# A decoder block with two token mixers: convolution taps summed in PSUM, one bank per chunk for the recurrence, and one merge for all chunks

## The chip, the cores and the metric

The kernel runs on one core of a Trainium2 chip. A core has a matrix engine (PE, with weight loads shown apart as PEld), a vector engine (DVE), an activation engine (ACT), a general engine (POOL) and an engine that here only issues DMAs (SP). SBUF is the working memory; PSUM is the small memory in eight banks that PE writes its products to. Each engine runs its own instructions in the order in which they were written for it.

The metric is the device time of one execution in microseconds (us), as the median of several runs. A lower time is better.

## The reference

One residual block on x (2048 tokens of 1024 channels), in float32. All widths are 1024, the recurrence has 16 heads of 64.

```python
h = _rmsnorm(x, norm_g) * (1 + scale) + shift           # scale, shift, gate from c
p = h @ w_in                                            # 1024 -> 9344
c_val, c_gate, c_og, ts, r_og, g_conv, g_rwkv = split(p)

# branch A: gated causal depthwise convolution of width 31
u = c_val * sigmoid(c_gate)
u = causal_depthwise_conv(u, conv_k) + conv_b
y_conv = (silu(layernorm(u)) * silu(c_og)) @ w_conv_out

# branch B: RWKV-7, per head a 64 x 64 state
r, k, v, w_low, a_low = split(token_shift(ts))
state = state * w_t - (state @ kk_t) b_t^T + v_t k_t^T  # for each token t
o_t = state @ r_t
y_rwkv = ((groupnorm(o) + (r * k * r_k).sum() * v) * silu(r_og)) @ w_rwkv_out

m = sigmoid(g_conv) * y_conv + sigmoid(g_rwkv) * y_rwkv
out = _rmsnorm(x + gate * (m @ w_out), final_g)
```

## The kernel before

**Tiling.** The 2048 tokens are worked in 4 blocks of 512 (b). In a block, the normalised input lies as 8 tiles of 128 channels by 512 tokens, each split into a high and a low part, so that a product of float32 is three fast matmuls (mm3k, L173). Within a block, the 16 heads are worked in 4 groups (g) of 4 heads, two pairs of heads each; so there are 16 groups in all.

**A group** (function group) does the following in turn.
1. pair (L420), once for each of the two pairs, makes the decayed keys and queries of the 8 chunks of 64 tokens (KR, BK, tk) and the matrices between tokens of a chunk (As). uv holds the values, and later the solution beside them.
2. The inverse. Each chunk needs the inverse of a unit triangular 64 x 64 matrix. Its two 32 x 32 diagonal blocks are sent through DRAM (dA, then La) so that 128 of them lie one to a partition, two for each block. POOL runs 31 steps of elimination, each a product (L568) and a sum (L570) on 1 to 16 rows. The results go back through DRAM (dT, L574) into As by 16 DMAs on SP's queue (L581).
3. The merge (L583 to L610) makes the off-diagonal block. For e = 0 and 1 (even and odd chunks lie in different partitions): 16 transposes of 32 x 32 on DVE (T11, L591), 16 small matmuls into the bank late (L597), a copy to SBUF (Qs, L600), 16 more matmuls into late (L606), and two copies into As (L610). The pool pl has one bank under the tag late, which xnorm's transposes and the group's own output transposes (L683) use as well.
4. The chain over the chunks (L615 to L656). In chunk c: Se is the decayed state (ACT, L621); xo = KR x state (L624) plus the values' part (L629); X is its copy to SBUF by DVE (L632); the solution gd = inverse x X (L637); uv = gd x rn by DVE (L639); the state's update from tk x uv (L643) and four DVE instructions (L648); last the output o, added by matmuls to the other half of xo (L654), and copied by ACT into O (L656). xo has two buffers (pool px), gd has one bank of its own (pool pg). The next chunk needs the new state.
5. Group normalisation and the transposes of the output (L669 to L686).

**The convolution** (function conv) is run 8 times a block. Two projections give gate and value, u is their gated product with 30 tokens of history in front (L711). DVE sums the 31 taps: the first writes the tile yj in SBUF (L714), and 30 instructions each add one tap in place (L717). yj has one buffer and goes to DRAM by a DMA of SP (L719).

**Order.** The code is written group by group, with the convolutions and gate projections (fill) behind or between the parts of a group. A planner then orders the instructions of each engine once and for all, by priority, by when it reckons their inputs to be ready, and by free buffers. So the projections (L173) are laid between the steps of the chain, and the next group's pairs, inverse and transposes between the chunks of the one before. Where an input comes later than planned, the engine stands, and everything behind it on that engine with it. After the blocks a second phase (L850 on) makes the output projections.

The banks of PSUM during the blocks: pm 2 (main products), pa 2 (aux), px 2 (xo), pl 1 (late), pg 1 (gd).

Of the kernel before, what the change touches and what calls it, by code (L numbers as in the profile page):

```python
# [9 lines left out]
F32 = mybir.dt.float32  # L10
# [8 lines left out]
P = 128  # L19
# [63 lines left out]
def hybrid_block(ctx: ExitStack, tc: tile.TileContext, x, vecs, convk, w2a2, final_g, ada, w_in, w_co, w_ro, w_o, crow, out,  # L83
# [137 lines left out]
    pg = late.enter_context(tc.tile_pool(name="pg", bufs=1, space=PSUM))  # L221
# [120 lines left out]
    def hprep0(xs, ada_steps):  # L342
# [17 lines left out]
        for k in range(KT):  # L360
            next(ada_steps)
            pt = (pl, pg)[k % 2].tile([P, NTT, P], F32, name="ps_x", tag=("late", "gd")[k % 2])
# [52 lines left out]
    def vrow(e):  # L415
        return slice(0, 64) if e == 0 else slice(64, 128)
# [118 lines left out]
    def group(b, g, h, lora, fill):  # L535
# [48 lines left out]
        Qs = lt.tile([P, 2, 2, NCH // 2, 32], F32, name="Qs", tag="i2")  # L584
        for e in range(2):
            p0 = 64 - 64 * e
            lo_, hi_ = slice(p0, p0 + 32), slice(p0 + 32, p0 + 64)
            for q in range(2):
                for hh in range(2):
                    for c in range(NCH // 2):  # L590
                        nc.vector.transpose(T11[lo_, q, hh, c, :], As[q][lo_, hh, 2 * c + e, lo_])  # L591
            pq = pl.tile([P, 2, 2, NCH // 2, 32], F32, name="late", tag="late")
            n = 0
            for q in range(2):
                for hh in range(2):
                    for c in range(NCH // 2):
                        nc.tensor.matmul(pq[hi_, q, hh, c, :], As[q][lo_, hh, 2 * c + e, hi_], T11[lo_, q, hh, c, :],  # L597
                                         start=(n == 0), stop=(n == 15), skip_group_check=True)
                        n += 1
            nc.vector.tensor_copy(Qs[hi_], pq[hi_])  # L600
            pf = pl.tile([P, 2, 2, NCH // 2, 32], F32, name="late", tag="late")
            n = 0
            for q in range(2):
                for hh in range(2):
                    for c in range(NCH // 2):
                        nc.tensor.matmul(pf[lo_, q, hh, c, :], Qs[hi_, q, hh, c, :], As[q][hi_, hh, 2 * c + e, hi_],  # L606
                                         start=(n == 0), stop=(n == 15), skip_group_check=True)
                        n += 1
            for q in range(2):
                nc.vector.tensor_copy(As[q][lo_, :, e::2, hi_], pf[lo_, q])  # L610
# [3 lines left out]
        Sg = S[g]  # L614
        for c in range(NCH):  # L615
# [474 lines left out]
```

## Time and profile before

| | |
|---|---|
| median of 3 runs | 3379.35 us (3379.3 to 3392.31) |
| the profiled execution, its own time | 3373.04 us |
| its span, first to last instruction | 3371.3 us |
| mean granted clock of PE | 0.959 |
| instructions | 65315 |
| moved by DMA | 606.98 MB, mean 180 GB/s |

The span is the stretch from the first to the last instruction; the time of the execution has 1.7 us around it. In the profile a row of a group reads: line, engine, operation, tile written, arrow, tiles read, shape, count, then busy us and the mean ns of one, then the idle time of the engine just before such instructions and what ended it. An arrow with a name behind an idle time says whom the engine waited for. In the rows of stretches a number in brackets is a count of instructions. In the order of time, a row has its start, its length, and in square brackets the idle time before it. The four instruction names that matter most below are T (the tile T11), late (the merge's bank), yj (the taps) and gd, X, xo, uv, S (the chain). The tile's name there lacks its number, so T11 is T.

### The profile page before, as it was taken

The numbers are of one execution on the slowest core, as the hardware profiler recorded it, in microseconds if no ns is written. First come the engines' busy times: TensorE is split into PE (matmuls) and PEld (weight loads), VectorE is DVE, ScalarE is ACT, GpSimd is POOL, SyncE is SP. The second block draws the span as 40 slices with busy tenths as digits, with TensorE's granted clock in tenths as the row PEclk, the third lists the DMA queues.
The fourth block names the chain that finished last, engine by engine and source line by source line (L and its number), as shares of the span: only waits on it lengthen the run. The fifth ranks groups of instructions, "written<-read, shape, count | busy, mean of one in ns | idle before, by whom it ended". The sixth has DMA issues, their size and how long they took to land.

```text
span 3371.3 us, 65315 instructions
## 1 busy us (share of the span) xinstructions
PE 3110.2 (92%) x25664; PEld 2874.4 (85%) x25664; DVE 2378.0 (71%) x4712; ACT 1063.8 (32%) x1900; POOL 1587.6 (47%) x2158
## 2 busy tenths in 40 slices
PE   6889898999999989999999899999989898878998
PEld 5789898888899988898989898989989877667887
DVE  7786777776677665767666567757688656889755
ACT  4432433332223131323232314132322223344422
POOL 3375454534544535253636355727576413746201
PEclk9999999999999999899999999999999999898999
DMA  7765656663546465445554556646446655655543
GB/s 295 243 210 181 230 174 222 222 197 119 177 142 190 140 184 166 148 132 174 159 155 150 182 165 215 211 124 186 158 127 200 217 181 188 216 184 177 179 158 124
DMA packets 328468, 606.98 MB, mean 180 GB/s; under 512 B 130848, under 2 KB 147552, under 8 KB 328160
## 3 DMA queue, kind: packets, MB, share of 16 engines
q1 hardware_dynamic: 265088, 373.14, 33.7%
q0 software_dynamic: 63072, 229.67, 22.0%
q8 instruction: 202, 3.31, 0.4%
q14 instruction: 106, 0.87, 0.1%
HBM read 439.03 MB, written 162.53 MB: 178 GB/s over the span
## 4 chain that ended last, share of the span: by engine, by line
PE 46%; DVE 18%; POOL 15%; DMA 11%; issue 6%; SPq 2%; ACT 2%; POOLq 0%; DVEq 0%; ACTq 0%
PE ps_main L173 30%; POOL TT L570 5%; POOL itmp L568 5%; DVE yj L717 5%; PE aux L504 3%; DMA As<-dT 2%; DMA dT<-TT 2%; DMA La<-dA 1%; PE gd L637 1%; PE xo L654 1%; PE xo L629 1%; DMA dA<-As 1%; POOL w_lo L158 1%; PE gd L643 1%; PE pout L1007 1%
## 5 line engine op out<-in xcount | busy, mean ns | idle before, releaser
L173 PE MATMUL ps_main<-h_hi,w_hi 128*128 128x256 f32 x4608 | 981.0, 290 | 39.8 <-DVE th L700 18.0
L173 PE MATMUL ps_main<-h_hi,w_lo 128*128 128x256 f32 x4608 | 973.5, 289 | 26.4 <-POOL w_lo L158 24.4
L173 PE MATMUL ps_main<-h_lo,w_hi 128*128 128x256 f32 x4608 | 964.9, 288 | 0.2 <-DVE h_lo L328 0.2
L717 DVE SCALAR_TENSOR_TENSOR yj<-u,ck,yj 128x512 f32<-128x512 f32 x960 | 802.3, 836 | 21.8
L173 PEld LDWEIGHTS ps_main<-h_hi,w_hi 128*128 128x128 f32 x4608 | 732.0, 193 | 60.4 <-issue 21.5
L173 PEld LDWEIGHTS ps_main<-h_hi,w_lo 128*128 128x128 f32 x4608 | 730.7, 193 | 40.5 <-POOL w_lo L158 27.0
L173 PEld LDWEIGHTS ps_main<-h_lo,w_hi 128*128 128x128 f32 x4608 | 730.1, 193 | 8.2 <-issue 1.2
L568 POOL TENSOR_TENSOR itmp<-La,TT 128x126 f32<-128x126 f32 (+22 forms) x496 | 274.2, 553 | 105.1 <-DMA La<-dA 73.5
L156 ACT CAST w_hi<-w_st 128x1024 fp32r<-128x1024 f32 x167 | 175.5, 1051 | 446.5 <-DMA w_st<-w_in_t 114.7
L570 POOL TENSOR_TENSOR TT<-TT,itmp 128x126 f32<-128x126 f32 (+22 forms) x496 | 279.5, 564 | 32.7
L149 POOL DMA_DIRECT2D w_hi<-kh_in x219 | 126.8, 579 | 348.5 <-PE ps_main L173 323.9
L158 DVE TENSOR_TENSOR w_lo<-w_st,w_hi 128x1024 fp32r<-128x1024 f32 x120 | 162.9, 1357 | 132.8 <-PE ps_main L173 50.3
L648 DVE SCALAR_TENSOR_TENSOR S<-gd,pe,Se 64x64 f32<-64x64 f32 x512 | 144.7, 283 | 91.6 <-PE gd L643 82.6
L158 POOL TENSOR_TENSOR w_lo<-w_st,w_hi 128x1024 fp32r<-128x1024 f32 x47 | 117.8, 2506 | 94.8 <-ACT w_hi L156 91.2
L656 ACT COPY uv<-xo 64x256 f32<-64x256 f32 x128 | 47.1, 368 | 342.6 <-PE xo L654 270.4
L506 DVE TENSOR_TENSOR As<-aux,maskA 128x512 f32<-128x512 f32 x128 | 88.3, 691 | 86.1 <-PE aux L504 85.8
L1018 POOL TENSOR_TENSOR xt<-xt,tg 128x256 f32<-128x256 f32 x60 | 52.8, 901 | 199.2 <-DVE tg L1014 192.0
L522 POOL TENSOR_TENSOR vv<-rk,vv 128x512 f32<-128x512 f32 x32 | 45.2, 1412 | 210.6 <-PE aux L519 152.5
L504 PE MATMUL aux<-KR,BKz 128*128 128x128 f32 x1024 | 138.2, 279 | 3.1 <-ACT rk L492 2.3
L504 PEld LDWEIGHTS aux<-KR,BKz 128*128 128x128 f32 x1024 | 125.2, 191 | 7.3 <-ACT rk L492 2.8
L591 DVE STREAM_TRANSPOSE T<-As 32x32 f32<-32x32 f32 x512 | 58.0, 166 | 102.7 <-DMA As<-dT 101.5
L632 DVE COPY X<-xo 64x256 f32<-64x256 f32 x128 | 53.7, 420 | 102.8 <-PE xo L629 101.5
(293 smaller groups left out, 5867.1 us busy)
## 6 DMA issues: line engine op xcount, KB each, us to landing
w_hi<-kh_in POOLq DMA_DIRECT2D x219, 512.0 KB, 4.0
w_lo<-kl_in POOLq DMA_DIRECT2D x219, 512.0 KB, 5.1
w_st<-w_in_t SPq DMA_DIRECT2D x73, 512.0 KB, 4.6
kh_in<-w_hi SPq DMA_DIRECT2D x71, 512.0 KB, 3.1
kl_in<-w_lo SPq DMA_DIRECT2D x71, 512.0 KB, 3.9
w_st<-w_ro_t SPq DMA_DIRECT2D x32, 512.0 KB, 4.0
w_st<-w_co_t SPq DMA_DIRECT2D x32, 512.0 KB, 3.8
w_st<-w_o_t SPq DMA_DIRECT2D x32, 512.0 KB, 3.6
```

Of the source, the lines that this page charges most:

```text
L149: nc.gpsimd.dma_start(hi, back[0])
L156: nc.scalar.copy(hi, st)
L158: lo_eng.tensor_tensor(out=lo, in0=st, in1=hi.bitcast(F32), op=ALU.subtract)
L173: nc.tensor.matmul(ps[:, qs], ww[:, k, :], aa[k][:, qs], start=(k == 0 and t == 0 and q == 0), stop=(k == KT - 1 and t == 2 and q == ms - ...
L504: nc.tensor.matmul(pA[:, c // 2, es], BKz[:, hh, cc, es], KR[:, cc, es], start=(c == 0), stop=(c == 3), skip_group_check=True)
L506: nc.vector.tensor_tensor(out=Asb[:, hh, c4 * 4:c4 * 4 + 4, :].rearrange("p (a e) n -> p a (e n)", e=2), in0=pA, in1=flat(maskA).unsqueeze ...
L568: nc.gpsimd.tensor_tensor(out=tmp[:, :ni, :nt], in0=La[:, j:j + 1, j + 1:].broadcast_to([P, ni, nt]), in1=TT[:, :ni, j:j + 1].broadcast_to ...
L570: nc.gpsimd.tensor_tensor(out=TT[:, :ni, j + 1:], in0=TT[:, :ni, j + 1:], in1=tmp[:, :ni, :nt], op=ALU.add)
L591: nc.vector.transpose(T11[lo_, q, hh, c, :], As[q][lo_, hh, 2 * c + e, lo_])
L632: nc.vector.tensor_copy(X[pr_], xo[pr_])
L648: nc.vector.scalar_tensor_tensor(out=Sg[hs, q, hs], in0=gd[hs, 2 + q, hs], scalar=R[q]["pe"][hs, c:c + 1], in1=Se[hs, q, hs], op0=ALU.mult ...
L717: nc.vector.scalar_tensor_tensor(out=yj, in0=u[:, i:i + TB], scalar=ck[:, j, i:i + 1], in1=yj, op0=ALU.mult, op1=ALU.add)
```

## The change

Four edits in the same diff.

- **Taps.** A pool pc of one PSUM bank takes the place of pg. The first tap writes its tile acc, the next 29 add in place in acc, and the last reads acc and writes yj in SBUF. The transposes of the first block (hprep0), which borrowed pg's bank, borrow acc's.
- **One bank per chunk.** xo grows from two to four columns blocks of 128, which is a whole bank. The solution and the state's update, which were in gd, now go into xo: the solution over the part that X was copied from, the update into the two new blocks.
- **Output.** The matmuls and the copy of o are put into a function olast, which is called for chunk c in chunk c + 1, between the copy to X and the solution, and after the loop for the last chunk.
- **Merge.** The loop over e that held everything is split into stages, each for both e: first all transposes, now one for four chunks at a time (32 x 128 instead of four of 32 x 32); then 32 matmuls; two copies to Qs; 32 matmuls; four copies into As. All of it uses one tile in late.

```diff
-    pg = late.enter_context(tc.tile_pool(name="pg", bufs=1, space=PSUM))
+    pc = late.enter_context(tc.tile_pool(name="pc", bufs=1, space=PSUM))
...
-            pt = (pl, pg)[k % 2].tile([P, NTT, P], F32, name="ps_x", tag=("late", "gd")[k % 2])
+            pt = (pl, pc)[k % 2].tile([P, NTT, P], F32, name="ps_x", tag=("late", "acc")[k % 2])
...
+        def quarters(e):
+            p0 = 64 - 64 * e
+            return slice(p0, p0 + 32), slice(p0 + 32, p0 + 64)
+        every = [(q, hh, c) for q in range(2) for hh in range(2) for c in range(NCH // 2)]
+        pq = pl.tile([P, 2, 2, NCH // 2, 32], F32, name="late", tag="late")
         for e in range(2):
-            p0 = 64 - 64 * e
-            lo_, hi_ = slice(p0, p0 + 32), slice(p0 + 32, p0 + 64)
+            lo_, hi_ = quarters(e)
             for q in range(2):
                 for hh in range(2):
-                    for c in range(NCH // 2):
-                        nc.vector.transpose(T11[lo_, q, hh, c, :], As[q][lo_, hh, 2 * c + e, lo_])
-            pq = pl.tile([P, 2, 2, NCH // 2, 32], F32, name="late", tag="late")
...
+                    nc.vector.transpose(T11[lo_, q, hh], As[q][lo_, hh, e::2, lo_])
+        for e in range(2):
+            lo_, hi_ = quarters(e)
+            for n, (q, hh, c) in enumerate(every):
+                nc.tensor.matmul(pq[hi_, q, hh, c, :], As[q][lo_, hh, 2 * c + e, hi_], T11[lo_, q, hh, c, :],
+                                 start=(n == 0), stop=(n == 15), skip_group_check=True)
+        for e in range(2):
+            lo_, hi_ = quarters(e)
+            nc.vector.tensor_copy(Qs[hi_], pq[hi_])
+        for e in range(2):
+            lo_, hi_ = quarters(e)
+            for n, (q, hh, c) in enumerate(every):
+                nc.tensor.matmul(pq[lo_, q, hh, c, :], Qs[hi_, q, hh, c, :], As[q][hi_, hh, 2 * c + e, hi_],
+                                 start=(n == 0), stop=(n == 15), skip_group_check=True)
+        for e in range(2):
+            lo_, hi_ = quarters(e)
+            for q in range(2):
+                nc.vector.tensor_copy(As[q][lo_, :, e::2, hi_], pq[lo_, q])
...
+        def olast(c, xo):
+            vr, rc = vrow(c % 2), rcol(c % 2)
             for q in range(2):
                 for hh in range(2):
+                    hs = slice(64 * hh, 64 * hh + 64)
+                    nc.tensor.matmul(xo[vr, q, hs], As[q][:, hh, c, rc], uv[:, c, q, hs],
+                                     start=False, stop=(q == 1 and hh == 1), skip_group_check=True)
+            nc.scalar.copy(O[vr, c // 2], xo[vr, 0:2])
...
-            xo = px.tile([P, 2, P], F32, name="xo", tag="xo")
+            xo = px.tile([P, 4, P], F32, name="xo", tag="xo")
...
-            nc.vector.tensor_copy(X[pr_], xo[pr_])
-            gd = pg.tile([P, 4, P], F32, name="gd", tag="gd")
+            nc.vector.tensor_copy(X[pr_], xo[pr_, 0:2])
+            if prev:
+                olast(*prev)
...
-                    nc.tensor.matmul(gd[pr_, q, hs], As[q][pr_, hh, c, kcol(e)], X[pr_, q, hs],
+                    nc.tensor.matmul(xo[pr_, q, hs], As[q][pr_, hh, c, kcol(e)], X[pr_, q, hs],
...
-                nc.tensor.matmul(gd[:, 2 + q, :], R[q]["tk"][:, c, :], uv[:, c, q, :], start=(q == 0), stop=(q == 1),
+                nc.tensor.matmul(xo[:, 2 + q, :], R[q]["tk"][:, c, :], uv[:, c, q, :], start=False, stop=(q == 1),
...
-            for q in range(2):
-                for hh in range(2):
-                    hs = slice(64 * hh, 64 * hh + 64)
-                    nc.tensor.matmul(xo[vr, q, hs], As[q][:, hh, c, rcol(e)], uv[:, c, q, hs],
-                                     start=False, stop=(q == 1 and hh == 1), skip_group_check=True)
-            nc.scalar.copy(O[vr, cc], xo[vr])
+            prev = (c, xo)
+        olast(*prev)
...
-        nc.vector.tensor_scalar(out=yj, in0=u[:, HALO:], scalar1=ck[:, j, HALO:HALO + 1], scalar2=vc("conv_b", j),
+        acc = pc.tile([P, TB], F32, name="acc", tag="acc")
+        nc.vector.tensor_scalar(out=acc, in0=u[:, HALO:], scalar1=ck[:, j, HALO:HALO + 1], scalar2=vc("conv_b", j),
                                 op0=ALU.mult, op1=ALU.add)
         for i in range(HALO):
-            nc.vector.scalar_tensor_tensor(out=yj, in0=u[:, i:i + TB], scalar=ck[:, j, i:i + 1], in1=yj,
-                                           op0=ALU.mult, op1=ALU.add)
+            nc.vector.scalar_tensor_tensor(out=acc if i + 1 < HALO else yj, in0=u[:, i:i + TB],
+                                           scalar=ck[:, j, i:i + 1], in1=acc, op0=ALU.mult, op1=ALU.add)
```

More of the change, by code (lines that the diff above doesn't have):

```diff
@@ L594, in group @@
+        O = uv[:, 0::2]
+        Sg = S[g]
+        prev = None
+        def olast(c, xo):
+            vr, rc = vrow(c % 2), rcol(c % 2)
             for q in range(2):
                 for hh in range(2):
[L596 to L599, printed above, removed]
@@ L600, in group @@
-            nc.vector.tensor_copy(Qs[hi_], pq[hi_])
-            pf = pl.tile([P, 2, 2, NCH // 2, 32], F32, name="late", tag="late")
-            n = 0
-            for q in range(2):
-                for hh in range(2):
[L605 to L608, printed above, removed]
```

11 lines of the change are left out of this document (2 added, 9 removed).

## The prediction

> **What bounds the kernel now.** I read the page first: the share of each engine, then PE over the span, then the chain that ended last.
>
> ```profile
> span 3371.3 us, 65315 instructions
> ...
> PE 3110.2 (92%) x25664; PEld 2874.4 (85%) x25664; DVE 2378.0 (71%) x4712; ACT 1063.8 (32%) x1900; POOL 1587.6 (47%) x2158
> ...
> PE   6889898999999989999999899999989898878998
> ...
> PE 46%; DVE 18%; POOL 15%; DMA 11%; issue 6%; SPq 2%; ACT 2%; POOLq 0%; DVEq 0%; ACTq 0%
> ```
>
> PE is busy 3110 of 3371 us, and no matmul is added or dropped by the change. So whatever the other engines win, the time can fall only by idle time of PE, 261 us in all. The second view is the busy time by stretch, to see where that idle time lies. The columns are PE, PEld, DVE, ACT and POOL busy, the clock, and DMA.
>
> ```profile
> 0.00:152.00 152.00, 111.35 (x848) 102.46 (x848) 105.52 (x232) 68.74 (x116) 42.04 (x46) 0.98 0.75 272
> 152.00:2700.00 2548.00, 2400.41 (x21473) 2257.91 (x21473) 1802.40 (x3755) 752.95 (x1369) 1310.30 (x1936) 0.96 0.56 175
> 2700.00:3371.00 671.00, 598.43 (x3345) 514.06 (x3344) 470.11 (x727) 242.08 (x416) 235.24 (x176) 0.94 0.53 177
> ```
>
> Taps, inverse, merge and the chunk chain run between 152 and 2700 us (the last chain ends a little later). There PE idles 2548 - 2400 = 148 us. The 41 us at the start and the 73 us at the end are of code that the change hardly touches. So about 148 us is at stake, 4.4% of the span. The third view is the waits of PE:
>
> ```profile
> PE gd L643 <- DVE uv L639: 24.9, 7, 9.2
> PE ps_main L173 <- POOL w_lo L158: 24.4, 13, 4.6
> ...
> PE ps_main L173 <- DVE th L700: 18.0, 5, 10.4
> PE late L597 <- DVE T L591: 15.9, 9, 3.3
> PE aux L249 <- ACT rh L490: 12.4, 6, 6.6
> ...
> PE ps_main L173 <- DVE carry L401: 9.1, 8, 1.9
> ...
> PE gd L637 <- DVE X L632: 6.7, 6, 2.9
> PE xo L624 <- DVE S L648: 6.4, 5, 3.8
> ```
>
> Columns: total us, times, longest. The largest wait is for the product uv, an instruction of DVE of 0.4 us that was late by up to 9.2 us. Why it was late shows in the order of time around that place, for DVE, then POOL, SP and PE:
>
> ```profile
> 1178.47 2.31 DVE L717 SCALAR_TENSOR_TENSOR yj<-u,ck,yj 128x512 f32<-128x512 f32 x3
> 1189.17 0.96 DVE L591 STREAM_TRANSPOSE T<-As 32x32 f32<-32x32 f32 x8 [8.39 <-DMA As<-dT]
> 1194.77 0.48 DVE L591 STREAM_TRANSPOSE T<-As 32x32 f32<-32x32 f32 x4 [4.63 <-DMA As<-dT]
> 1195.18 0.37 DVE L639 TENSOR_TENSOR uv<-gd,rn 64x256 f32<-64x256 f32 x1
> ```
>
> ```profile
> 1171.03 0.36 POOL L568 TENSOR_TENSOR itmp<-La,TT 128x91 f32<-128x91 f32 x1
> 1171.47 0.38 POOL L570 TENSOR_TENSOR TT<-TT,itmp 128x91 f32<-128x91 f32 x1
> ...
> 1175.56 0.28 POOL L568 TENSOR_TENSOR itmp<-La,TT 128x56 f32<-128x56 f32 x1
> ...
> 1178.40 0.93 POOL L570 TENSOR_TENSOR TT<-TT,itmp 128x30 f32<-128x30 f32 x1
> ```
>
> ```profile
> 1187.59 8.90 SPq L581 DMA_DIRECT2D As<-dT  x16
> ```
>
> ```profile
> 1195.60 1.22 PE L643 MATMUL gd<-uv,tk 128*128 128x128 f32 x4 [9.16 <-DVE uv L639]
> ```
>
> Each engine runs its instructions in the order written by the planner. The transposes of the merge stand on DVE ahead of the other group's uv, and wait for DMAs that start only when POOL's inverse has ended. So a late inverse blocks DVE, and DVE blocks PE. The inverse itself is slow exactly while taps (L717) run: 0.28 us for 56 elements without a tap beside it, 0.93 us for 30 with one.
>
> **The change part by part.**
>
> *Taps in PSUM (L714, L717).* 960 taps keep count and order. One SBUF input (yj) and the output move to PSUM; the output of the 30th tap stays in SBUF.
>
> ```profile
> L717 DVE SCALAR_TENSOR_TENSOR yj<-u,ck,yj 128x512 f32<-128x512 f32 x960 | 802.3, 836 | 21.8
> L568 POOL TENSOR_TENSOR itmp<-La,TT 128x126 f32<-128x126 f32 (+22 forms) x496 | 274.2, 553 | 105.1 <-DMA La<-dA 73.5
> L570 POOL TENSOR_TENSOR TT<-TT,itmp 128x126 f32<-128x126 f32 (+22 forms) x496 | 279.5, 564 | 32.7
> L714 DVE TENSOR_SCALAR yj<-u,ck,v 128x512 f32<-128x512 f32 x32 | 20.7, 648 | 14.6 <-DMA y_d<-yj 13.7
> L600 DVE COPY Qs<-late 32x512 f32<-32x512 f32 x32 | 22.1, 690 | 32.6 <-PE late L597 32.1
> ```
>
> ```profile
> L717 DVE SCALAR_TENSOR_TENSOR yj<-u,ck,yj x960: 695/752/2862, 152.3 to 2665.1; 128x512 f32<-128x512 f32 x192
> ```
>
> ```profile
> L397 DVE SCALAR_TENSOR_TENSOR vv<-ps_main,v,t x31: 726/750/751, 115.1 to 2535.3; 128x511 f32<-128x511 f32 x31
> ```
>
> Min/median/max of a tap are 695/752/2862 ns. The same operation with one input in PSUM and a column as scalar (L397) takes 726/750/751: as long, but without the tail. No row shows DVE writing PSUM, so I bound it: below by the fastest tap, 695 ns; above by what a PSUM side costs a plain copy, L600's 690 against L714's mean of 648 at the same length, put on the present mean: 836 + 42 = 878. I take 750, L397 being the nearest row. DVE then saves 960 x (836 - 750) = 83 us (between 135 saved and 40 lost). The first tap may rise from 648 to 690: 32 x 0.04 = 1 us. Its wait for the store of yj (13.7 us) moves to the 30th tap, at least 29 x 0.75 = 22 us later, and is gone.
>
> If the tail of the taps comes from POOL reading SBUF beside them, POOL gains too. The 31 steps of the inverse have (j//2 + 1)(31 - j) elements, 92 on average, so the 128x91 rows are its mean shape: free, 31 x (0.36 + 0.38) = 23 us; now, 31 x (0.553 + 0.564) = 35 us. That is at most 12 us an inverse; other DVE work beside POOL stays, so I take 8.5 us. A late inverse then ends 8.5 us earlier, its DMAs and transposes too. The uv waits (longest 9.2) shrink to about 0.7 in all, T's 15.9 to none, and th's longest, 10.4, to 1.9: 24.2 + 15.9 + 8.5 = 49 us. Of w_lo (24.4, POOL's queue) and of carry and rh (21.5, DVE's queue) I take a quarter, 11 us.
>
> [...]
>
> *Banks.* The accumulator takes the bank of gd, and xo grows within its own bank: two plus one either way. The first block's transposes merely change the tag. Nothing.
>
> *The chain.* A chunk issues the same matmuls. The eight passes of o (L654) and their ACT copy move from behind the S update into the next chunk, between the X copy and the solution.
>
> ```profile
> L654 PE MATMUL xo<-uv,As 128*64 128x64 f32 x1024 | 89.6, 233 | 0.0
> L632 DVE COPY X<-xo 64x256 f32<-64x256 f32 x128 | 53.7, 420 | 102.8 <-PE xo L629 101.5
> ```
>
> o takes 89.6/128 = 0.70 us a chunk, the X copy 0.42: where nothing else stands between, the solution comes 0.28 us later, and the S update loses a cover of 0.70. Projections cover both nearly everywhere: PE waited for X in 6 chunks of 128 and for S in 5. So 6 x 0.28 + 5 x 0.7 = 5 us lost; all uncovered it would be 125 us, which those counts exclude. xo is held half a chunk longer; with two buffers the chunk after next waits for ACT's copy, a copy of a quarter of a bank with the rest of a chunk to do it in. Behind that copy on ACT stand Se and the splits; ACT is 32% busy.
>
> *The merge.* 32 transposes of 32x32 a group become 8 of 32x128, and four uses of the one late bank become one.
>
> ```profile
> L591 DVE STREAM_TRANSPOSE T<-As 32x32 f32<-32x32 f32 x512 | 58.0, 166 | 102.7 <-DMA As<-dT 101.5
> ```
>
> ```profile
> L597 PE MATMUL late<-T,As 32*32 32x32 f32 x1024 | 43.1, 195 | 18.6 <-DVE T L591 15.9 <-ACT xsq L305 2.4 <-ACT oc L685 0.3
> ```
>
> Upper bound 4 x 166 ns (no gain); lower, from copies of 256 and 512 elements (420 and 690 ns, 1.05 ns an element), 0.166 + 96 x 0.00105 = 0.27 us. I take that: 128 x 0.27 = 34 us, 24 us less of DVE. Fewer hand-overs between PE and DVE help the first chunk; PE hardly waits there beyond the T row already counted, so 0. The first copy of Qs may wait for the products of both halves, 43.1/32 = 1.3 us more; behind it on DVE stand the other chain's X, uv and S, and two later hand-overs go for it. And all eight transposes now stand ahead of the first product, and the last needs the 14th of the 16 DMAs where half of them needed the 10th: 4 x 8.90/16 = 2.2 us more in which DVE stands. With the inverse earlier I count nothing for it; uncovered it is a rival.
>
> **Sum.** 49 + 11 - 5 = 55 us less idle PE. A stall that goes uncovers the next (the DMAs' own path, POOL's uv at L683), so I take 50. The profiled execution took 3373.04 us (span 3371.3 plus 1.7 around it), 6.3 under the median of the runs, 3379.35. So 3373 - 50 = 3323 in its terms, 3329 against the median.
>
> **Rivals.**
> 1. *More than that*: the whole idle time behind DVE and POOL's w_lo in the waits above goes (24.9 + 24.4 + 18.0 + 15.9 + 12.4 + 9.1 + 6.7 + 6.4 = 118): 3261. For: all hang on two overfull queues. Against: it takes every one of these waits to zero, those too whose releaser the change does not touch.
> 2. *Hidden*: the plan is remade, its transposes sit at other places, and PE meets as many late instructions as now: within 17 us of 3379. For: PE is busy 94% of the stretch. Against: the stalls come from one late event.
> [...]
> 4. *The merge blocks DVE for longer*, the slow side: 16 x 2.2 = 36 us if a chain step stands behind the transposes in each group, as at 1189 us: 3379 + 36 = 3415, without the gain from POOL; half of it 3397. It decides where the DMAs still land after DVE has reached the transposes, so where the inverse does not get about 2.2 us faster. For: T now waits 101.5 us in 35 places for DMAs. Against: the rows of POOL.
>
> **How the numbers follow.** Forecast (3295 to 3360) 0.52, rival 1 0.10, rival 2 0.13, rival 3 0.08, rival 4 0.17. Faster by over 0.5% (about what a measurement can tell from no change, 17 us): 0.52 + 0.10 = 0.62; within: 0.13; slower: 0.25. The range goes from the middle between rival 1 and the forecast's end, about 3275, to 3402, past half the price of rivals 3 and 4. The forecast's own range is 3295 to 3360.
>
> **What would show it.** Right: taps near 750 ns with a maximum under 900; L568 and L570 at about 0.42 us mean; uv and T waits of PE a few us; PE idle in the middle near 100 us. The merge: transposes near 0.27 us. The chain: no new PE wait for X. [...]

## The result and the profile after

The changed kernel takes **3229.35 us** (median of 4 runs, 3226.71 to 3237.57). The kernel before took 3382.87 us on the same chip (median of 4, 3379.3 to 3392.31). The ratio is 0.9546, with a 95% interval of 0.9518 to 0.9574: 4.5% faster, some 153 us. The forecast was 3329, its range 3275 to 3402. The sign was right, and the time lies below the whole range.

The profiled execution took 3226.71 us, 146 less than that of before. First the page of the kernel after: span, engines, PE over the span, and the chain that ended last.

```profile
span 3225.0 us, 64867 instructions
...
PE 3040.3 (94%) x25664; PEld 2832.5 (88%) x25664; DVE 2305.3 (71%) x4328; ACT 1062.0 (33%) x1900; POOL 1386.1 (43%) x2158
...
PE   6899999999999999899999998999989998688998
...
PE 69%; DVE 14%; DMA 8%; issue 3%; POOL 3%; ACT 3%; SPq 1%; DVEq 0%; POOLq 0%; ACTq 0%
```

POOL fell from 15% of the chain to 3%, and PE rose from 46% to 69%. The number to stop at is PE's own busy time: 3110.2 before, 3040.3 now, with the same 25664 matmuls. The forecast had taken it as fixed. Next the busy time by stretch. The middle now ends at 2550 us, since everything comes sooner.

```profile
0.00:152.00 152.00, 111.95 (x856) 103.19 (x857) 109.01 (x239) 69.33 (x117) 43.24 (x49) 0.98 0.76 276
152.00:2550.00 2398.00, 2325.80 (x21405) 2211.22 (x21405) 1718.60 (x3359) 747.75 (x1363) 1101.46 (x1931) 0.98 0.60 186
2550.00:3225.00 675.00, 602.55 (x3411) 518.06 (x3407) 477.67 (x731) 244.89 (x420) 241.35 (x179) 0.94 0.53 177
```

In the middle PE idles 2398 - 2326 = 72 us instead of 148. Its start and end idle as before (40 and 72 us). So the span lost 76 us of idle time and 70 us of busy time: 146 together.

The waits of PE after (total us, times, longest) show which idle time went:

```profile
PE aux L249 <- ACT rh L490: 37.7, 12, 9.1
...
PE ps_main L173 <- DVE carry L401: 9.1, 9, 2.0
...
PE xo L642 <- DVE S L667: 4.5, 2, 3.1
...
PE ps_main L173 <- DVE th L715: 3.2, 2, 2.8
...
PE xo L662 <- DVE uv L658: 3.0, 4, 1.7
PE ps_main L173 <- POOL w_lo L158: 3.0, 3, 1.6
...
PE xo L656 <- DVE X L650: 2.8, 1, 2.8
```

Before, uv had 24.9, w_lo 24.4, th 18.0, T 15.9 (no longer in the list), X 6.7. All are down to about 3 or less. Of the waits that the prediction listed one grew: that for rh, from 12.4 to 37.7. Outside its list rs (L123) grew from 7.1 to 16.7 and DVE's w_lo (L158) from 5.9 to 15.2.

The groups that the taps touch, from the view by line (busy us, mean ns of one, idle before):

```profile
L733 DVE SCALAR_TENSOR_TENSOR acc<-u,ck,acc 128x512 f32<-128x512 f32 x928 | 697.9, 752 | 23.5
...
L570 POOL TENSOR_TENSOR TT<-TT,itmp 128x126 f32<-128x126 f32 (+22 forms) x496 | 189.6, 382 | 34.1
L568 POOL TENSOR_TENSOR itmp<-La,TT 128x126 f32<-128x126 f32 (+22 forms) x496 | 181.0, 365 | 107.8 <-DMA La<-dA 75.4
...
L730 DVE TENSOR_SCALAR acc<-u,ck,v 128x512 f32<-128x512 f32 x32 | 26.0, 812 | 1.1
```

And the spread of the taps (ns, min/median/max):

```profile
L733 DVE SCALAR_TENSOR_TENSOR acc<-u,ck,acc x928: 696/756/959, 150.7 to 2488.8; 128x512 f32<-128x512 f32 x186
```

The tail of the taps is gone (2862 before, 959 now). POOL's two steps fell from 553 and 564 to 365 and 382 ns, on the same tiles.

**Where the 70 us of PE's busy time came from.** Two things are in it. The first is the clock. The views of cores of before and after:

```profile
core 0: 3371.3 us, clock 0.959
```

```profile
core 0: 3225.0 us, clock 0.970
```

The clock records of the trace have two levels, 1 and 0.5. The half-clock stretches add up to 279 us in 44 pieces before, and to 198 us in 30 pieces after; 0.041 x 3371.3 = 138 and 0.030 x 3225.0 = 97 are about half of them. What such a stretch costs shows behind the 9.16 us stall that ended at 1195.6 us in the kernel before, in the view of stretches; PE is busy throughout in both rows, and the column to read is its count of matmuls, then the clock:

```profile
1195.70:1200.50 4.80, 4.80 (x27) 4.46 (x28) 4.65 (x19) 1.44 (x3) 0.00 (x0) 0.57 0.23 68
1200.70:1205.50 4.80, 4.80 (x43) 4.80 (x42) 4.76 (x14) 1.21 (x3) 2.48 (x3) 1.00 0.39 82
```

In 4.80 us PE did 27 matmuls just after the stall, about a dozen of them the short ones of tk and o, and 43 a little later, all projections. Both count as busy. So such a stall is paid as idle time first and as busy time after.

That this is no single case shows in the clock records. In both kernels they change only at multiples of 3.41 us from one another. In the kernel before there are 45 windows of that length, between two such points, in which PE idled for 2.0 us or more, and after every one of them the next window is at half clock; of the 851 windows with less than 0.5 us of idle time, 14 have such a successor. In the kernel after it is 25 of 25, and 8 of 843.

The second is what a change of the matmul's tile shape costs. In order of time for PE, before (start, length, count):

```profile
1008.97 0.60 PE L643 MATMUL gd<-uv,tk 128*128 128x128 f32 x4
1009.50 0.68 PE L654 MATMUL xo<-uv,As 128*64 128x64 f32 x8
1010.11 0.39 PE L173 MATMUL ps_main<-h_hi,w_hi 128*128 128x256 f32 x1
```

and after, at two places of a chunk:

```profile
1347.79 0.60 PE L662 MATMUL xo<-uv,tk 128*128 128x128 f32 x4
1348.15 0.36 PE L173 MATMUL ps_main<-h_hi,w_hi 128*128 128x256 f32 x1
1348.35 0.40 PE L173 MATMUL ps_main<-h_lo,w_hi 128*128 128x256 f32 x2
...
1352.93 0.68 PE L647 MATMUL xo<-uv,As 64*64 64x64 f32 x8
1353.53 0.68 PE L627 MATMUL xo<-uv,As 128*64 128x64 f32 x8
1354.14 0.71 PE L504 MATMUL aux<-KR,BKz 128*128 128x128 f32 x4
```

Read the starts, not the lengths. Four matmuls of tk occupied PE for 0.53 us when o (tile 128*64) came behind them, and for 0.36 us when a projection (128*128) did. Not all of the 0.17 us is won: the projection behind tk takes 0.20 us to the next start, where one in a row of projections takes 0.12. The eight of o take 0.61 us to the next start in both places. Now o stands behind the values' part (L647), which is of a small shape already, in 112 of 128 chunks. So PE leaves the shape 128*128 and comes back to it twice in such a chunk, and not three times.

I summed over PE's records each matmul's time to the next start, or to its own end where PE then idled, apart for the two clocks. Half-clock time in it is 215.3 us before and 145.5 after, 70 us less. Taken as half lost that is worth 35 us; a projection takes 213 ns from start to start at half clock and 118 at full clock (medians), and by this ratio it is 31. With half-clock time counted half, tk fell by 23 us, the merge's matmuls by 9, and KR x state by 3: 35 us; the projections rose by 4, and the rest fell by as much. Together that is the 70.

### The profile page after: what moved, and what is told of

Read it like the earlier page. It is cut to its first block, busy times and chain, and to the rows that moved or that the text cites. A ratio compares the mean times of both kernels' runs of the same rounds, so it can differ in the third digit from the quotient of the medians.

```text
span 3225.0 us, 64867 instructions
## 1 busy us (share of the span) xinstructions
PE 3040.3 (94%) x25664; PEld 2832.5 (88%) x25664; DVE 2305.3 (71%) x4328; ACT 1062.0 (33%) x1900; POOL 1386.1 (43%) x2158
## 4 chain that ended last, share of the span: by engine, by line
PE 69%; DVE 14%; DMA 8%; issue 3%; POOL 3%; ACT 3%; SPq 1%; DVEq 0%; POOLq 0%; ACTq 0%
PE ps_main L173 47%; PE aux L504 3%; DMA w_st<-w_in_t 3%; PE xo L656 2%; PE xo L647 2%; PE xo L627 2%; PE xo L642 2%; PE pout L1024 2%; PE xo L662 2%; PE pout L1023 2%; PE pout L1025 2%; DVE acc L733 1%; DMA As<-dT 1%; ACT w_hi L156 1%; PE late L609 1%
## 5 line engine op out<-in xcount | busy, mean ns | idle before, releaser
L733 DVE SCALAR_TENSOR_TENSOR acc<-u,ck,acc 128x512 f32<-128x512 f32 x928 | 697.9, 752 | 23.5
L149 POOL DMA_DIRECT2D w_hi<-kh_in x219 | 126.2, 576 | 526.6 <-PE ps_main L173 497.0
L158 DVE TENSOR_TENSOR w_lo<-w_st,w_hi 128x1024 fp32r<-128x1024 f32 x120 | 164.9, 1374 | 115.1 <-PE ps_main L173 45.2
L568 POOL TENSOR_TENSOR itmp<-La,TT 128x126 f32<-128x126 f32 (+22 forms) x496 | 181.0, 365 | 107.8 <-DMA La<-dA 75.4
L667 DVE SCALAR_TENSOR_TENSOR S<-xo,pe,Se 64x64 f32<-64x64 f32 x512 | 144.7, 283 | 93.1 <-PE xo L662 82.7
L637 ACT ACTIVATE Se<-S,pe 128x128 f32<-128x128 f32 x256 | 89.1, 395 | 357.9 <-DVE S L667 357.6
L570 POOL TENSOR_TENSOR TT<-TT,itmp 128x126 f32<-128x126 f32 (+22 forms) x496 | 189.6, 382 | 34.1
L158 POOL TENSOR_TENSOR w_lo<-w_st,w_hi 128x1024 fp32r<-128x1024 f32 x47 | 112.9, 2401 | 112.9 <-ACT w_hi L156 89.2
L658 DVE TENSOR_TENSOR uv<-xo,rn 64x256 f32<-64x256 f32 x128 | 53.8, 421 | 120.5 <-PE xo L656 119.7
L150 POOL DMA_DIRECT2D w_lo<-kl_in x219 | 119.3, 545 | 18.9 <-PE ps_main L173 11.1
```

Of the source, the lines that this page charges most:

```text
L149: nc.gpsimd.dma_start(hi, back[0])
L150: nc.gpsimd.dma_start(lo, back[1])
L158: lo_eng.tensor_tensor(out=lo, in0=st, in1=hi.bitcast(F32), op=ALU.subtract)
L568: nc.gpsimd.tensor_tensor(out=tmp[:, :ni, :nt], in0=La[:, j:j + 1, j + 1:].broadcast_to([P, ni, nt]), in1=TT[:, :ni, j:j + 1].broadcast_to ...
L570: nc.gpsimd.tensor_tensor(out=TT[:, :ni, j + 1:], in0=TT[:, :ni, j + 1:], in1=tmp[:, :ni, :nt], op=ALU.add)
L637: nc.scalar.mul(Se[:, q, :], Sg[:, q, :], R[q]["pe"][:, c:c + 1])
```

## The experiments

The theory: the taps' two reads of SBUF slow POOL's inverse, and moving one of them to PSUM carries most of the gain. The rival: the new order of the chain and the merge carry it. All ratios are against the kernel before on the same chip. All other columns are of the one profiled execution: PE busy, PE idle and half-clock time (us); POOL, the mean of the first and of the second step of the inverse (ns); out, when PE's first matmul of the output phase starts (us); idle to out, how long PE idles from 152 us to then.

| kernel | ratio (95% interval) | median us | PE busy | PE idle | half clock | POOL | out | idle to out |
|---|---|---|---|---|---|---|---|---|
| before | 1 | 3379 to 3387 | 3110 | 250 | 279 | 553, 564 | 2706 | 150 |
| after | 0.9546 (0.9518 to 0.9574) | 3229.35 | 3040 | 173 | 198 | 365, 382 | 2564 | 74 |
| taps back in SBUF | 0.9901 (0.9888 to 0.9915) | 3350.21 | 3071 | 261 | 281 | 513, 554 | 2681 | 155 |
| o back home | 0.9604 (0.959 to 0.9618) | 3249.02 | 3069 | 176 | 224 | 361, 381 | 2594 | 78 |
| old merge | 0.9567 (0.9554 to 0.958) | 3235.37 | 3048 | 172 | 190 | 365, 377 | 2570 | 72 |
| scaling on ACT | 0.9494 (0.9479 to 0.9509) | 3212.57 | 3048 | 159 | 192 | 368, 380 | 2557 | 59 |
| only o moved | 1.0008 (0.9993 to 1.0023) | 3384.84 | 3132 | 249 | 316 | 546, 566 | 2722 | 147 |
| only the chain | 0.9979 (0.9964 to 0.9994) | 3374.08 | 3093 | 258 | 303 | 526, 543 | 2693 | 148 |
| only the merge | 0.9993 (0.9979 to 1.0008) | 3377.69 | 3104 | 255 | 295 | 538, 561 | 2696 | 143 |
| POOL refilled | 0.9705 (0.968 to 0.973) | 3281.77 | 3070 | 205 | 268 | 368, 386 | 2606 | 98 |
| DVE load, one SBUF input | 0.9685 (0.9662 to 0.9708) | 3273.81 | 3063 | 200 | 269 | 363, 381 | 2606 | 99 |
| DVE load, two SBUF inputs | 0.9852 (0.9828 to 0.9875) | 3330.56 | 3079 | 243 | 326 | 456, 448 | 2671 | 145 |
| taps alone | 0.9665 (0.964 to 0.9689) | 3270.57 | 3078 | 177 | 227 | 357, 383 | 2589 | 73 |

PE idle here counts up to PE's last matmul, so it is some 11 us less than span minus busy. A profiled execution need not be the middle one: that of the kernel after was the shortest of its four, those of o back home, POOL refilled, scaling on ACT and the load with two SBUF inputs the longest of theirs.

The last column sorts the kernels. In those without added work, whatever the chain and the merge look like, PE idles 143 to 155 us there with the taps in SBUF, and 72 to 78 with them in PSUM (59 with the scaling on ACT too).

**Taps back in SBUF.** The kernel after, with the taps as before.

```diff
-        acc = pc.tile([P, TB], F32, name="acc", tag="acc")
-        nc.vector.tensor_scalar(out=acc, in0=u[:, HALO:], ...
+        nc.vector.tensor_scalar(out=yj, in0=u[:, HALO:], ...
-            nc.vector.scalar_tensor_tensor(out=acc if i + 1 < HALO else yj, ..., in1=acc, ...
+            nc.vector.scalar_tensor_tensor(out=yj, ..., in1=yj, ...
```

> The changed kernel with the taps' sum back in SBUF; chain and merge stay changed. Theory (taps beside POOL slow the inverse, a late inverse blocks DVE, DVE blocks PE, and PE runs at half clock after each stall): taps back at a mean near 836 ns, L568 and L570 near 550 ns, PE idle between 150 us and the end of the blocks up by 50 to 76 us, PE busy up by 25 to 35 us, so 3305 to 3340 us. Rival (the chain in one bank and the single merge carry the gain): the POOL rows go up but the time stays within 15 us of 3229.

Its groups (same columns as above):

```profile
L732 DVE SCALAR_TENSOR_TENSOR yj<-u,ck,yj 128x512 f32<-128x512 f32 x960 | 804.4, 838 | 24.2
L570 POOL TENSOR_TENSOR TT<-TT,itmp 128x126 f32<-128x126 f32 (+22 forms) x496 | 274.6, 554 | 33.8
L568 POOL TENSOR_TENSOR itmp<-La,TT 128x126 f32<-128x126 f32 (+22 forms) x496 | 254.6, 513 | 86.5 <-DMA La<-dA 54.0
```

It takes 3350.21 us: 121 us of the gain are lost with this one edit, more than the theory had expected. Taps, POOL and PE's idle time return together nearly to what they were before. The other edits keep 34 us, and since idle time (261) is no less than before and half-clock time (281) the same, those lie in PE's busy time at full clock.

**Taps alone.** The kernel after, with the old merge, and o in its own chunk; the chain keeps its one bank, which the taps' bank needs.

```diff
-            if prev:
-                olast(*prev)
...
+            olast(c, xo)
...
-                    nc.vector.transpose(T11[lo_, q, hh], As[q][lo_, hh, e::2, lo_])
+                    for c in range(NCH // 2):
+                        nc.vector.transpose(T11[lo_, q, hh, c, :], As[q][lo_, hh, 2 * c + e, lo_])
```

> The taps in PSUM without the other two parts as far as that goes: the merge of before, o traced behind the state's update of its own chunk; the chain keeps one bank, since the accumulator needs gd's. Chain alone gave 8 us and merge alone 4 of 155. Theory (the taps carry nearly all of it, chain and merge little by themselves): 3240 to 3275 us, POOL's inverse near 370 ns a step, PE idle 170 to 190 us. Rival (the taps' gain comes only together with the new merge or with o's new place): 3300 us or more.

It takes 3270.57 us, 117 below the kernel before on its chip, as the theory had it. So the taps carry about three quarters of the gain, measured from both ends (121 and 117). The edit is not the taps wholly alone: with the one bank, o no longer stands right behind tk in any chunk. By the sum from start to start tk fell from 74.0 to 50.9 us and KR x state rose from 66.9 to 74.3, so some 16 of the 117 us are the chain's.

**o back home, and old merge.** The kernel after with one edit undone each. The first:

```diff
-            if prev:
-                olast(*prev)
...
-            prev = (c, xo)
-        olast(*prev)
+            olast(c, xo)
```

> The changed kernel with o's matmuls back behind the state's update of the same chunk; one bank a chunk, taps in PSUM and one merge stay. Theory (a matmul of another tile shape costs PE a switch: 205 ns from tk to o before, 31 ns from tk to a projection after, and o now stands behind the values' part, which has a small shape too): PE busy up by 20 to 28 us, of it tk's share from 48 back to about 74 us, so 3249 to 3260 us. Rival (where o stands is free, PE does the same matmuls): within 8 us of 3229.

The second puts back the lines of the merge of before, 32 transposes and two banks in turn:

```diff
-        pq = pl.tile([P, 2, 2, NCH // 2, 32], F32, name="late", tag="late")
         for e in range(2):
...
+            pq = pl.tile([P, 2, 2, NCH // 2, 32], F32, name="late", tag="late")
...
+            pf = pl.tile([P, 2, 2, NCH // 2, 32], F32, name="late", tag="late")
```

> The changed kernel with the merge of before (two halves in turn, 512 transposes); taps and chain stay changed. Theory (the merge is a side matter: 24 us of DVE, a few switches of PE): 3225 to 3245 us. Rival (the single use of the late bank and the fewer transposes ahead of the chain steps free DVE and PE, and are a main part of the gain): over 3260 us, with waits of PE for uv and T11 back.

With o home the kernel is 20 us slower and PE 28 us busier (in profiled executions that lie 31 apart), as expected, but the price does not lie where it was expected. tk's time to the next start stays at 48 us; the planner put o ahead of the next chunk's KR x state. KR after, in the view by line and form:

```profile
L642 PE MATMUL xo<-S,KR 128*128 128x128 f32 x512 | 97.1, 278 | 4.7 <-DVE S L667 4.5
```

and with o home:

```profile
L642 PE MATMUL xo<-S,KR 128*128 128x128 f32 x512 | 108.9, 299 | 1.7 <-DVE S L665 1.7
```

KR pays 12 us, and the clock about 13 (26 us more at half clock). The old merge costs 6 us by the medians (3235.37 and 3229.35). That is in the range of the theory, but the two intervals overlap, so it is not told apart from nothing.

**Only o moved.** The kernel before, with the function olast and its call between X and the solution; gd stays in its bank.

```diff
             nc.vector.tensor_copy(X[pr_], xo[pr_])
+            if prev:
+                olast(*prev)
             gd = pg.tile([P, 4, P], F32, name="gd", tag="gd")
```

> The kernel before with one part alone: o's matmuls and copy moved into the next chunk between X and the solution, gd keeps its bank, taps and merge as before. Theory (small shapes side by side save PE switches, and stalls by late taps stay): PE busy 15 to 28 us less at the same half-clock time, tk's group near 79 us from 82.9, time 3355 to 3370 us. Rival (as the prediction had it, PE does the same matmuls and waits a little more for X and S): 3380 to 3395 us.

It takes the time of the kernel before, which the rival had. But the edit did not do what it says: with gd apart, nothing holds o back, and the planner still issued it right behind tk in all 128 chunks. The run says nothing on the price of the shape; the next one does.

**Only the chain.** The kernel before with olast and its call, and with gd's work in xo, as in the change; taps in SBUF, old merge.

```diff
+            if prev:
+                olast(*prev)
...
-                    nc.tensor.matmul(gd[pr_, q, hs], As[q][pr_, hh, c, kcol(e)], X[pr_, q, hs],
+                    nc.tensor.matmul(xo[pr_, q, hs], As[q][pr_, hh, c, kcol(e)], X[pr_, q, hs],
```

> The kernel before with one part alone: the chain in one bank a chunk with o in the next chunk; taps in SBUF, merge of before, so the accumulator's bank is left unused. In the run with gd kept, o went on standing directly behind tk; with one bank it can't, as the update's reads of that bank come first. Theory (the new neighbours of o save PE 0.17 us a chunk in switches of tile shape, and the late inverse stays): PE busy 20 to 30 us less, o behind the values' part, 3350 to 3365 us. Rival (the gain of 34 us with taps in SBUF is the merge's): within 10 us of 3383.

Here o does follow the values' part, in 112 chunks. tk's time to the next start is 52.6 us (74.0 before), and PE is busy 17 us less. The time fell by 8 us only, less than the theory had, and within the rival's range. Its waits of PE (columns as above):

```profile
PE aux L249 <- ACT rh L490: 36.7, 10, 16.9
PE ps_main L173 <- DVE mr L921: 33.3, 4, 22.5
...
PE xo L653 <- DVE X L647: 16.8, 8, 4.8
PE xo L639 <- DVE S L664: 15.6, 7, 4.5
```

X had 6.7, S 6.4, rh 12.4 and mr 1.6 in the kernel before. In the blocks the waits changed places: those for X, S and rh grew, and uv fell to 2.5, th to 5.3 and T to none although POOL's inverse is about as slow as before (526 and 543 ns). PE's idle time up to the output phase stayed (148 us against 150), and that phase starts 12 us sooner. Behind that, the output phase, which the edit does not touch, has one wait of 22.5 us for mr.

**Only the merge.** The kernel before with the new merge.

```diff
...
-                    for c in range(NCH // 2):
-                        nc.vector.transpose(T11[lo_, q, hh, c, :], As[q][lo_, hh, 2 * c + e, lo_])
+                    nc.vector.transpose(T11[lo_, q, hh], As[q][lo_, hh, e::2, lo_])
...
```

> The kernel before with one part alone: the merge for all chunks at once; taps in SBUF, gd and o as before. Theory (24 us of DVE and a few switches of PE): 3365 to 3383 us, PE's share of the merge from 77 to about 68 us. Rival of the prediction (all eight transposes stand ahead on DVE and wait for DMAs that a late inverse sends late): 3390 to 3420 us, T11's wait for the DMAs over 101 us. The other rival (it carries most of the 34 us of chain and merge): 3350 to 3360 us.

It takes 3377.69 us, no difference that can be told. DVE's wait for the DMAs ahead of the transposes is 87.4 us against 101.5, so the blocking that was feared did not come either. Alone, chain and merge give 8 and 4 us; together (taps back in SBUF) 34. That does not add up by the whole time, but it does up to the output phase: it starts 12 us sooner with the chain, 10 with the merge, and 25 with both. Here too the output phase holds one wait of 22.5 us for mr.

**POOL refilled.** The kernel after, with a memset ahead of each product of the inverse, so that POOL's inverse takes about as long as before while the taps stay in PSUM. The memset's values are overwritten.

```diff
+            nc.gpsimd.memset(tmp.rearrange("p a b -> p (a b)")[:, 0:340], 0.0)
             nc.gpsimd.tensor_tensor(out=tmp[:, :ni, :nt], in0=La[:, j:j + 1, j + 1:].broadcast_to([P, ni, nt]),
```

> The changed kernel with a POOL memset of 128x340 before each of the 31 products of every inverse, some 0.35 us each, so that POOL's inverse is again about 11 us longer, as with taps in SBUF, but the planner knows of it and DVE loses nothing. Theory (it is the lateness against the plan that stalls DVE and PE): within 20 us of 3229. Rival (the length of the inverse itself bounds the groups): PE idle up by 50 us or more, 3285 to 3320 us.

```profile
L568 POOL MEMSET itmp<- 128x340 f32 x496 | 191.0, 385 | 48.3 <-PE late L601 24.8
```

This row of the view by line gives 191 us more of POOL, 12 us an inverse. DVE's busy time stays as it was (2306 us). It costs 52 us, where the theory had allowed 20; that is close under the rival's range, with 32 us more of PE's idle time instead of the rival's 50. The planner knows of these memsets and can make room; they still cost 0.27 us for each us of POOL. So a good part of what the taps brought is the length of the inverse itself.

**DVE loaded, with one and with two SBUF inputs.** The kernel after with 384 more instructions between the taps, whose results are overwritten. In the first, their second input is acc in PSUM:

```diff
+            if i % 5 in (1, 3):
+                nc.vector.scalar_tensor_tensor(out=yj, in0=u[:, i:i + TB], scalar=ck[:, j, i:i + 1], in1=acc, ...
```

> The changed kernel with 12 more instructions of a tap's kind in each convolution (384 in all, their result is overwritten by the last tap), with one input in PSUM: some 288 us more of DVE, three and a half times what the taps' move saved. Theory (DVE's load is not what was bought): 0.75 us each, POOL's inverse unchanged near 370 ns, time 3235 to 3275 us. Rival (the 83 us of DVE saved are the gain of the taps): at least 3229 + 120, 3350 us or more.

In the second it is u, in SBUF:

```diff
-                nc.vector.scalar_tensor_tensor(out=yj, in0=u[:, i:i + TB], ..., in1=acc, ...
+                nc.vector.scalar_tensor_tensor(out=yj, in0=u[:, i:i + TB], ..., in1=u[:, i:i + TB], ...
```

> The same 384 further instructions, but with both inputs in SBUF. Theory (two inputs in SBUF beside POOL is the whole difference): they take 0.84 us on average, L568 and L570 rise from 370 to about 430 to 450 ns by 12/30 of what the taps cost them, and the time is 25 to 60 us above the kernel with the input in PSUM. Rival (a DVE instruction is a DVE instruction, or the accumulator's bank mattered): within 12 us of it.

The added instruction (L736) and POOL's steps, with the input in PSUM:

```profile
L736 DVE SCALAR_TENSOR_TENSOR yj<-u,ck,acc 128x512 f32<-128x512 f32 x384 | 285.1, 742 | 25.2 <-DMA y_d<-yj 17.0
L570 POOL TENSOR_TENSOR TT<-TT,itmp 128x126 f32<-128x126 f32 (+22 forms) x496 | 189.0, 381 | 33.9
L568 POOL TENSOR_TENSOR itmp<-La,TT 128x126 f32<-128x126 f32 (+22 forms) x496 | 180.2, 363 | 136.5 <-DMA La<-dA 103.7
```

and in SBUF:

```profile
L736 DVE SCALAR_TENSOR_TENSOR yj<-u,ck 128x512 f32<-128x512 f32 x384 | 312.9, 815 | 7.4 <-DMA y_d<-yj 4.3
...
L568 POOL TENSOR_TENSOR itmp<-La,TT 128x126 f32<-128x126 f32 (+22 forms) x496 | 226.3, 456 | 101.2 <-DMA La<-dA 68.2
L570 POOL TENSOR_TENSOR TT<-TT,itmp 128x126 f32<-128x126 f32 (+22 forms) x496 | 222.4, 448 | 33.5
```

This pair isolates the second SBUF input. Count, shape and place in the program of the added work are the same, and so are all other instructions as they are written; only one input lies elsewhere, and the planner is free to order the two differently. POOL slows from 363 and 381 to 456 and 448 ns, the instruction itself from 742 to 815, and the kernel by 57 us (3273.81 to 3330.56); the loss lies in the range expected of the theory. What holds POOL up beside such an instruction was not shown. The first of the pair also gives a price of DVE time alone. Its rows add up to 285 us, but rows overlap, and DVE's busy time rose by 202 us. That cost 44 us, within the range of its theory and far from its rival: 0.22 us for each. The price is an upper one, since the added instructions also waited 17.0 us for the store of yj.

**Scaling on ACT.** The wait for rh is what grew. rh follows rk (L487) on DVE, and at 1310 us of the kernel after a pair of instructions of the next block's normalisation stands ahead of it:

```profile
1310.12 4.57 DVE L312 TENSOR_SCALAR xt<-xt,ss 128x512 f32<-128x512 f32 x2
```

The kernel after with these 24 instructions on ACT, which is 33% busy:

```diff
-                nc.vector.tensor_scalar(out=xh[kh], in0=xh[kh], scalar1=rs, scalar2=None, op0=ALU.mult)
+                nc.scalar.mul(xh[kh], xh[kh], rs)
```

> The changed kernel with the scaling of x in xnorm (L312) moved from DVE to ACT, for the other blocks' normalisation. In the changed kernel two such DVE instructions took 4.57 us beside POOL at 1310 us, and PE then waited 9.1 us for rh. Theory (what blocks DVE beside POOL comes out as idle PE and half clock): the wait of PE for rh falls from 37.7 to 15 to 30 us, time 3205 to 3225 us. Rival (the next late instruction takes its place, or ACT becomes late): within 8 us of 3229.

```profile
PE aux L249 <- ACT rh L490: 1.6, 1, 1.6
```

In its waits of PE, rh fell from 37.7 to 1.6, and a wait for T came back (10.0). The kernel takes 3212.57 us (3204.7 to 3219.62), and its interval lies below that of the change: the fastest version of this study. PE's busy time did not fall with it (3048, in the longest of its four executions).

## Why the prediction was wrong: right in the mechanism, blind to PE's own time

**The step that failed** is the second sentence under the first view: no matmul is added or dropped, "so whatever the other engines win, the time can fall only by idle time of PE". 70 of the 146 us came out of PE's busy time, of which the forecast had none. With the 76 us of idle time alone the time would have been 3379 - 76 = 3303, inside its range. About half of the 70 is time at half clock, which fell with the windows of 2.0 us of idle time or more (45 before, 25 after); the other half is fewer costly changes of shape, most of it behind tk, with smaller sums at the merge and KR.

**The sum of idle time** was 49 + 11 - 5 = 55 us, measured 76. Of the 49: uv to 3.0 (0.7 forecast), T to none (as forecast), th to 3.2 (1.9 forecast). Of w_lo, carry and rh a quarter was taken; w_lo alone gave 21.4, carry nothing, and rh lost 25.3. X and S gave 6 where 5 were to be lost. The waits that the sum names so changed by 53 - 4 + 6 = 55 in all, which is what was forecast, but by luck: two of its parts missed by 15 and 11. The other 21 us came out of waits that it does not name, that for POOL's uv (L678), 9.8 us before and 0.5 after, among them.

To cost a wait by its name was the weaker part of it. With the chain alone changed, uv, th and T fell as well, while the inverse was about as slow as before and PE idled as long. So the second rival had a point: the plan is remade, and its waits change places. What stays is their sum up to the output phase, and that follows the taps: 150 us before, 155 with the taps back in SBUF, 73 with the taps alone.

**Taps.** Taken 750 ns, measured 752, with a maximum of 959 (the sign was to be under 900). DVE fell by 73 us in all, of which the taps have 48 (against taps back in SBUF) to 64 (taps alone); 83 were forecast. The added instructions, out of PSUM into SBUF, took 742 ns. The first tap, which only writes PSUM, cost more than forecast: 812 ns against 690, 5 us instead of 1.

**POOL.** Taken 8.5 us an inverse, under a bound of 12. Measured (188 + 182) x 31 ns = 11.5 us. The bound held. How the 8.5 us turned into time was too narrow: they were subtracted from the longest of a wait, as if only the latest inverse mattered. Lengthening all 16 inverses by 12 us, with the planner told of it, costs 52 us.

**The chain.** Costed at 5 us of lost time. The waits for X and S fell instead (to 2.8 and 4.5), but with the chain alone they rose to 16.8 and 15.6, 19 us more, so the fall is not the chain's. In place of a loss stands a gain of about 20 us (o back home) that was not seen.

**The merge.** Taken 0.27 us a transpose; after, the 128 transposes have a median of 299 ns. Worth 4 to 6 us, neither of them clear of noise. The matmuls of the merge gained 9 us on PE, which was costed at 0.

**Rivals.** The first (3261, all idle behind late DVE and POOL gone) was nearest, and still 32 too high, since it too counts idle time only. The second fell with PE's idle time, though not with the waits by name. The third (taps at 878 ns or more) fell with the taps' 752 ns. No run shows the 878, on which its chance of 0.08 and half of its price (960 x 42 ns = 40 us) in the upper end of the range, 3402, rest; the runs showed 752 ns in the kernel after, and 836 and 838 with the taps in SBUF. The fourth (the merge blocks DVE) fell too: DVE's wait for the DMAs ahead of the transposes, 101.5 us before, is down to a third. It is the taps that do it: the wait is 93.0 with the new merge and the taps back in SBUF, and 34.0 with the old merge and the taps in PSUM. Its row in the waits of DVE after (total us, times, longest):

```profile
DVE T L596 <- DMA As<-dT: 31.9, 22, 4.3
```

**What stays open.** How the taps' 120 us split. At the measured rates the 48 to 64 us of DVE are worth 0.22 times that, 11 to 14. The two steps of the inverse fell by 159 (against taps back in SBUF) to 187 us (taps alone). At the refill's 0.27 that is worth 43 to 50. The pair with one and two inputs, where the planner knows nothing of the slowing, gives 57 us, of which 34 us more of DVE explain 7; the other 50 stand against 79 us more of POOL, 0.63 for each. Between 0.27 and 0.63 the taps' POOL time is worth 43 to 118 us. That being later than planned costs more than being long is argued from these two rates and not shown by a run of its own. Nor was the half clock isolated by a run: that it goes with the stalls is read from the windows of the records. And every edit makes the planner lay all later work anew, the output phase too, where single waits of up to 24 us come and go; each kernel has one trace, so it is not known whether they stand in every execution.

## What to carry to other kernels

Do not take an engine's busy time as fixed because its instruction count is: look at its clock behind each stall (0.57 behind the one of 9.16 us here), and at the time from start to start where it changes tile shape (205 ns from tk to o, 111 from tk to tk). When a stream of two-input vector instructions runs beside another engine that reads the same memory, price what it does to that other engine too (456 and 448 ns for POOL's steps here, 363 and 381 with one input in PSUM), and put the accumulator in PSUM if a bank is free. When a plan is remade, do not follow single waits by name: compare the bounding engine's idle time phase by phase. A stall in a part that the edit does not touch, 22.5 us here, can hide what the edit won.

## What the runs showed of the hardware that was not expected

- **A stall is paid again as half clock.** In the rows above, 27 matmuls in 4.80 us at 0.57 against 43 at 1.00. The pieces at half clock in the records last 3.4 to 13.7 us, in steps of 3.41 but for the one that each trace ends with (9.46 and 9.92 us). Behind a window of 3.41 us with 2.0 us or more of idle time the next was at half clock each time (45 of 45 and 25 of 25), behind one with 0.5 to 2.0 us sometimes (20 of 81 and 22 of 66). In order of time for PE in the kernel after:

```profile
1341.67 0.78 PE L656 MATMUL xo<-X,As 64*64 64x64 f32 x8 [0.97 <-DVE As L614]
...
1343.24 0.79 PE L173 MATMUL ps_main<-h_hi,w_hi 128*128 128x256 f32 x2 [0.23 <-DVE carry L401]
1343.84 0.63 PE L173 MATMUL ps_main<-h_lo,w_hi 128*128 128x256 f32 x2
...
1347.19 0.40 PE L173 MATMUL ps_main<-h_lo,w_hi 128*128 128x256 f32 x2
```

Behind idle stretches of 0.97 and 0.23 us (and small matmuls before them), a pair takes 0.63 us, 3.4 us later 0.40.
- **A change of tile shape costs PE on both sides of it.** Medians from start to start at full clock in the kernel before: a matmul of tk takes 111 ns ahead of its own shape and 205 ahead of o, the last of a small shape 148 to 152 ahead of 128*128 and 58 inside its group, the first of a small shape 107, and a projection 225 behind a small shape and 118 in a row. So one trip out of 128*128 and back costs an estimated 0.34 us by these medians. From 64*64 to 128*64 it is a change too (148 and 107 in the kernel after); two small groups side by side save a trip, an estimated 0.2 us in all by the same medians.
- **A one-input vector instruction can be slow too.** L312 reads one SBUF tile; it took 475 ns at best and, in the row quoted above, 4.57 us for two. Beside it POOL issued DMAs and made a product of two SBUF tiles (L149, L150, L478). No run isolates why.
